# A four-layer mixer trunk on one core: first feed-forward blocks and three mLSTM heads projected down by Strassen's seven products

## The chip, the cores and the metric

The kernel runs on one core of a Trainium2 chip. The metric is the device time of one execution in microseconds, from its start to its end, with all inputs and the output in device memory. The engines are named as in the profile: PE is TensorE (matrix products), PEld its weight loads, DVE is VectorE, ACT is ScalarE, POOL is GpSimd and SP is SyncE, which here only issues DMAs.

## The reference

The trunk has two layers over 512 frames of 1024 features in float32. Each layer is a half-step feed-forward, a mixer, a second half-step feed-forward and a gated embedding, each followed by a residual sum and a layer norm:

```python
x = layer_norm(DN_ALPHA * x + 0.5 * swiglu_ffn(x, ffn1_wgu[i], ffn1_wd[i]), ...)
mix = mlstm_mixer(...) if i % 2 == 0 else gmlp_mixer(...)
x = layer_norm(DN_ALPHA * x + mix, ...)
x = layer_norm(DN_ALPHA * x + 0.5 * swiglu_ffn(x, ffn2_wgu[i], ffn2_wd[i]), ...)
x = layer_norm(DN_ALPHA * x + sigmoid(x @ ple_wg[i] + ple_bg[i]) * (p[i] @ ple_wp[i]), ...)

def swiglu_ffn(x, w_gu, w_d):            # 1024 -> 2 x 2816 -> 1024
    g, u = jnp.split(x @ w_gu, 2, axis=-1)
    return (jax.nn.silu(g) * u) @ w_d
```

The mLSTM mixer of layer 0 projects x to q and k (4 heads of 256 features each, a causal convolution of four taps and silu on them), v and z (4 heads of 512) and eight gate columns. Per head it forms gated causal scores of q and k, multiplies them by v, normalises by the scores' sum and then over the head's 512 features, and gates with norm_g and sigmoid(z). The four heads side by side (2048 features) are multiplied by `w_out` (2048 x 1024). The "down" of this document is the product with `w_d` or `w_out`, whose result is added to the residual stream. The gMLP mixer of layer 1 has a down projection of the same shape, which the change leaves alone.

## The kernel before, in words

**Numbers.** A float32 product is made of three products in the faster type fp32r: each operand is split into a high part and the rest, and `mm3` (L261) issues high x high, low x high and high x low (L263, L264, L265; in the changed kernel the same rows are L268 to L270). `split` (L267) writes the high part by a copy on ScalarE and the low part by a subtraction on VectorE. One "projection" is a weight tile of 128 columns by 1024 rows against all 512 frames, 24 matmuls of 512 columns into one bank of the accumulator memory. There are eight banks, four called "up" and four called "dn"; each pool hands its banks out in turn, and who gets a bank waits until its earlier reader is through.

**Weights.** The class `Weights` streams them in one fixed order for the whole program. A load brings up to 1 MB into a raw buffer (`wraw`, three of them) or, for the feed-forwards' down weights, half that into a quarter buffer (`wquarter`, five). `fill` (L163) then makes the split tiles `whi` (ScalarE) and `wlo` (VectorE; or, where `low="dma"` is passed, a negated copy on ScalarE and an accumulating DMA from GpSimd's queue) in rings of four "main" tiles and some extra ones. `take` hands the next tile to TensorE's code; `release` gives a ring slot back and thereby puts the split of a later tile into the instruction streams of ScalarE and VectorE at that place. `release(later=True)` keeps the slot back until `refill`.

**Order.** No scheduler moves anything: each engine runs its instructions in the order in which the Python code issues them. Engines meet only through semaphores on tiles and banks. So the place of a VectorE instruction in the code decides what it waits behind.

**Feed-forwards.** The 22 blocks of hidden features (128 each) are done in chunks of 2, 4, 4, 4, 4, 4 (`FFN_CHUNKS`). Per block there are two projections (gate and up), then silu and product into `h` or `hf`. The down product of a chunk runs while the next chunk is projected. Chunks 1 to 4 go by Strassen: `Group` views the chunk's `h` and its weights as 2 x 2 blocks and makes seven products, `gps`, one after each of the first seven projections of the next chunk. `form` prepares the left factor of a product (sums of blocks on VectorE, then a split into `fhi` and `flo`), `Weights.forms` the right factor (sums of raw weights in place, then `whi` and `wlo`). `product` runs 12 matmuls into one of two pairs of dn banks, even products into the first pair, odd ones into the second. `add` adds a product's two banks onto the residual `xt`; since products 2, 4, 5 and 6 add onto what already lies in the pair of banks, such a product may start only when the add before it on that pair has read it. The first and the last chunk go by the plain `down` (L591), 12 matmuls per block, frame quarter and pair of halves, tile name `dps`; the first chunk's down stands inside chunk 1 after two projections.

**mLSTM.** Per head: `project_qk` (four projections; per projection bias, convolution by one `TENSOR_SCALAR` L936 and three `SCALAR_TENSOR_TENSOR` L938, silu and a split), `project_v` (four frame quarters, each over four weight tiles, in dn banks), `scores` (24 matmuls into four banks, alternately up and dn; the gate factors `ex` on ScalarE; their product `sf` on VectorE, L1010; a split), two z projections, `mix` (scores times v in `nps`, normalisation up to `hn`, L1049), two more z projections, then the plain down of the head before (96 matmuls, 22 us of TensorE's time) and `gate_turn` (16 transposes into `hps`; product with `sz` into `hzf`, L1067; a split into `hh` and `hl`). In the last head the transposes stand between the frame quarters of that down, and after them comes the last head's own down, joined with the layer norm (`Norm`, whose vectors `g_bc` and `b_bc` have tiles of their own).

## Time and profile before

| | us |
|---|---|
| median of three runs (lowest, highest) | 2247.41 (2246.97, 2248.39) |
| the profiled execution | 2248.24 |
| its span in the trace | 2246.5 |
| first feed-forward (stages by the trace) | 0 to 364 |
| mLSTM | 364 to 778 |
| second feed-forward and embedding | 778 to 1191 |
| third feed-forward | 1191 to 1534 |
| gMLP | 1534 to 1837 |
| fourth feed-forward and embedding | 1837 to 2247 |

The profile is of one execution. A row of the trace in time order has the start and the duration in us, the engine, the line of the code, the instruction, its output and inputs by the program's names, and the shape; `x4` at its end means four such instructions in a row, and then the time is that of all four. A bracket, where there is one, is the idle time of the engine before it and what ended that. A row of the table by windows has the stretch, its length, then busy time and number of instructions in the order PE, PEld, DVE, ACT, POOL, then TensorE's granted clock (1.00 is full speed), the DMA engines' share and their GB/s; columns of engines that did nothing are left out in some rows. A row on waits has the waiting engine and tile, what it waited for, and the total in us, the number of waits and the longest. A row on DMAs has the tile, the queue, the number, the size of each and the median us from issue to landing.

### The profile page before, as it was taken

The numbers are of one execution on the slowest core, as the hardware profiler recorded it, in microseconds if no ns is written. First come the engines' busy times: TensorE is split into PE (matmuls) and PEld (weight loads), VectorE is DVE, ScalarE is ACT, GpSimd is POOL, SyncE is SP. The second block draws the span as 40 slices with busy tenths as digits, with TensorE's granted clock in tenths as the row PEclk, the third lists the DMA queues.
The fourth block names the chain that finished last, engine by engine and source line by source line (L and its number), as shares of the span: only waits on it lengthen the run. The fifth ranks groups of instructions, "written<-read, shape, count | busy, mean of one in ns | idle before, by whom it ended". The sixth has DMA issues, their size and how long they took to land.

```text
span 2246.5 us, 26356 instructions
## 1 busy us (share of the span) xinstructions
PE 2234.0 (99%) x10649; PEld 1875.2 (83%) x10649; DVE 1439.3 (64%) x2083; ACT 886.3 (39%) x1241; POOL 103.2 (5%) x136
## 2 busy tenths in 40 slices
PE   9999999999999999999999999999999999999998
PEld 8888888888888888888889888888888888888887
DVE  5566667765555656666687566666756566666677
ACT  3333336454544433333344333335344452333332
POOL 1000000111121000000000000000010100000000
PEclk9999999999999999999999999999999999999999
DMA  7322223376674534331333332222356453432221
GB/s 237 114 94 93 94 85 100 81 177 123 150 152 106 155 113 131 104 103 57 112 122 122 111 95 95 94 85 94 122 141 141 104 167 98 130 113 85 84 85 57
DMA packets 200754, 254.08 MB, mean 113 GB/s; under 512 B 5636, under 2 KB 155268, under 8 KB 200632
## 3 DMA queue, kind: packets, MB, share of 16 engines
q1 hardware_dynamic: 166864, 211.83, 29.1%
q0 software_dynamic: 27152, 25.87, 7.8%
q10 hardware_dynamic: 6616, 14.69, 2.0%
q8 instruction: 84, 1.38, 0.2%
q14 instruction: 38, 0.31, 0.0%
HBM read 224.58 MB, written 2.11 MB: 101 GB/s over the span
## 4 chain that ended last, share of the span: by engine, by line
PE 97%; DMA 1%; ACT 1%; issue 1%; DVE 0%; SPq 0%; POOL 0%; DVEq 0%; POOLq 0%
PE fps L265 13%; PE fps L263 13%; PE fps L264 13%; PE gps L265 6%; PE gps L263 6%; PE gps L264 6%; PE dps L264 5%; PE dps L265 5%; PE dps L263 5%; PE gups L263 1%; PE zps L263 1%; PE gvps L265 1%; PE zps L265 1%; PE gups L264 1%; PE gups L265 1%; PE zps L264 1%
## 5 line engine op out<-in xcount | busy, mean ns | idle before, releaser
L263 PE MATMUL fps<-xh,whi 128*128 128x512 f32 x1312 | 510.7, 389 | 0.0
L264 PE MATMUL fps<-xl,whi 128*128 128x512 f32 x1312 | 510.5, 389 | 0.0
L265 PE MATMUL fps<-xh,wlo 128*128 128x512 f32 x1312 | 510.4, 389 | 0.0
L194 DVE TENSOR_TENSOR wlo<-wraw,whi 128x1024 fp32r<-128x1024 f32 (+1 forms) x284 | 341.7, 1217 | 183.3 <-ACT whi L188 182.2
L188 ACT ACTIVATE whi<-wraw 128x1024 fp32r<-128x1024 f32 (+1 forms) x333 | 344.2, 1048 | 219.3 <-PE fps L264 103.2
L264 PEld LDWEIGHTS fps<-xl,whi 128*128 128x128 f32 x1312 | 246.3, 188 | 51.2
L265 PEld LDWEIGHTS fps<-xh,wlo 128*128 128x128 f32 x1312 | 246.3, 188 | 51.1
L263 PEld LDWEIGHTS fps<-xh,whi 128*128 128x128 f32 x1312 | 246.3, 188 | 50.9
L194 DVE TENSOR_TENSOR wlo<-wquarter,whi 128x1024 fp32r<-128x1024 f32 x112 | 137.2, 1225 | 202.1 <-ACT whi L188 202.1
L188 ACT ACTIVATE whi<-wquarter 128x1024 fp32r<-128x1024 f32 x112 | 118.7, 1060 | 237.8 <-PE gps L265 177.8
L265 PE MATMUL gps<-whi,flo 128*128 128x512 f32 x448 | 174.3, 389 | 0.0
L264 PE MATMUL gps<-wlo,fhi 128*128 128x512 f32 x448 | 174.3, 389 | 0.0
L263 PE MATMUL gps<-whi,fhi 128*128 128x512 f32 x448 | 174.3, 389 | 0.0
L790 ACT ACTIVATE sg<-fps 128x512 f32<-128x512 f32 x80 | 47.9, 598 | 280.8 <-PE fps L265 280.8
L565 DVE TENSOR_TENSOR xt<-xt,gps 128x512 f32<-128x512 f32 x224 | 143.0, 679 | 0.0
L268 ACT ACTIVATE fhi<-h 128x512 fp32r<-128x512 f32 x112 | 69.4, 625 | 115.9 <-DVE h L726 45.8
L263 PE MATMUL dps<-whi,hh 128*128 128x512 f32 x256 | 101.5, 396 | 0.0
L264 PE MATMUL dps<-wlo,hh 128*128 128x512 f32 x256 | 100.5, 393 | 0.0
L265 PE MATMUL dps<-whi,hl 128*128 128x512 f32 x256 | 100.3, 392 | 0.0
L269 DVE TENSOR_TENSOR flo<-h,fhi 128x512 fp32r<-128x512 f32 x112 | 75.6, 687 | 36.4 <-ACT fhi L268 36.4
L264 PEld LDWEIGHTS gps<-wlo,fhi 128*128 128x128 f32 x448 | 84.1, 188 | 17.5
L263 PEld LDWEIGHTS gps<-whi,fhi 128*128 128x128 f32 x448 | 84.1, 188 | 17.4
(277 smaller groups left out, 3852.4 us busy)
## 6 DMA issues: line engine op xcount, KB each, us to landing
wraw<-in_ffn_wgu_dram SPq DMA_DIRECT2D x79, 1024.0 KB, 5.4
wquarter<-in_ffn_wd_dram SPq DMA_DIRECT2D x64, 512.0 KB, 3.8
wlo<-wraw POOLq DMA_DIRECT2D x49, 512.0 KB, 7.6
wraw<-in_ml_w_in_dram SPq DMA_DIRECT2D x24, 1024.0 KB, 5.7
wraw<-in_gm_w_in_dram SPq DMA_DIRECT2D x15, 1024.0 KB, 5.6
wraw<-in_ffn_wd_dram SPq DMA_DIRECT2D x12, 1024.0 KB, 5.0
wraw<-in_ffn_wgu_dram SPq DMA_DIRECT2D x17, 512.0 KB, 3.9
wraw<-in_ml_w_out_dram SPq DMA_DIRECT2D x8, 1024.0 KB, 5.3
```

The source lines that it names most:

```text
L188: self.nc.scalar.activation(hi[:, s], src[:, s], AF.Copy)
L194: (low or self.nc.vector).tensor_sub(lo[:, s], src[:, s], hi[:, s].bitcast(F32))
L263: mm(ps, st[0], mv[0], start=start, stop=False, skip_group_check=more)
L264: mm(ps, st[0], mv[1], start=False, stop=False, skip_group_check=more)
L265: mm(ps, st[1], mv[0], start=False, stop=stop, skip_group_check=more)
L268: sca.activation(hi, src, AF.Copy)
L269: vec.tensor_sub(lo, src, hi.bitcast(F32))
L565: vec.tensor_add(dst, dst, ps)
L790: sca.activation(sg, ps, AF.Silu)
```

## The change

**Feed-forwards.** Chunk 0 becomes a `Group` too, with two blocks instead of four, so its 2 x 2 blocks are half as large: products of six matmuls, factors of 128 x 256. Its seven products stand after the first seven projections of chunk 1, as those of later chunks do. The first addition to `xt` scales the old residual by ALPHA; so in such a first group the products 0, 2, 3 and 6, which come to each of the four quarters of `xt` first, are added by `SCALAR_TENSOR_TENSOR` instead of `TENSOR_TENSOR`. The affine steps left over from the norm before run at the end of chunk 0 and after the first three projections of chunk 1.

**mLSTM.** Heads 0, 1 and 2 are written by `gate_turn` as plain float32 (`hf`), and a `Group` takes them down during the next head: `step` (add of the product before, the next product, release, next form) stands after the q/k projections 1, 2 and 3, after the v weight tiles 0, 1 and 3, and after the last z projection. The seven weight tiles of `w_out` stand among the head's twelve others by `ML_SLOTS`. One half of a head's `w_out` rows lies in one of the three raw buffers, which are now tracked one by one since they come free out of order, the other in a buffer shared with the norm's `g_bc` and `b_bc`. `project_v` of heads 1 to 3 runs over weight tiles outside and frame quarters inside, with the four up banks; their `scores` use the four up banks too, since the dn banks are pinned by the group. The third z projection moves into `mix` ahead of its last frame quarter. The low parts of z's weight tiles and of the tiles whose raw weights are changed in place no longer go by DMA. Head 3 goes down by the plain `down` with the norm; its transposes stand directly after its last z, with the last product of head 2 between the second and the third of them.

```diff
 class Weights:
-    def forms(self, quarter, kind, raw_kind):
+    def forms(self, kind, b11, b12, b22, b21):
...
+        for _, make in made:
+            self.in_place.add(make)
+        return [(kind, js, make) for js, make in made]
...
-                if low == "dma":
+                if low == "dma" and make not in self.in_place:
...
-                    (low or self.nc.vector).tensor_sub(lo[:, s], src[:, s], hi[:, s].bitcast(F32))
+                    self.nc.vector.tensor_sub(lo[:, s], src[:, s], hi[:, s].bitcast(F32))
...
+    ML_SLOTS = (1, 2, 3, 4, 5, 7, 11)
...
             if h:
-                o_w(h - 1)
-        o_w(HEADS - 1)
+                tiles = W.order[at:]
...
+                j0, j1 = W.add_load(kp(wout)[:, k:k + 2, :], 3), W.add_load(kp(wout)[:, k + 2:k + 4, :], 3, "gb")
...
+                for i, tile_i in enumerate(tiles):
+                    W.order.append(tile_i)
+                    if i in ML_SLOTS:
+                        W.order.append(down_w[ML_SLOTS.index(i)])
+        add_rows(wout, 4 * HEADS - 4, 4)
...
 class Group:
         def add(self):
             r = self.next_add
+            if r == self.next_product:
+                return
             self.next_add += 1
             i, j = self.TO[r]
             for e, ps in enumerate(self.banks[r % 2]):
-                residual(2 * i + e, j, ps, False)
+                residual(2 * i + e, j, ps, r in self.first)
+                if r >= 5:
+                    del pinned[id(ps)]
...
 def ffn:
             for c, n in enumerate(FFN_CHUNKS):
...
-                    if (c, i) in ((0, 3), (1, 0)):
+                    if c == 1 and i < 3:
                         run_affine()
-                    if i == 1 and pending is not None:
-                        down(pending, True)
...
-                if plain:
-                    pending = hs
-                else:
-                    group = Group(h, fpool)
+                if c < LAST:
+                    group = Group(h, fpool, c == 0)
                     group.form()
                     group.form()
+                if c == 0:
+                    run_affine()
...
 def project_qk:
                     W.release(low="dma")
+                    if i:
+                        step()
...
 def project_v:
+                banks = [up_bank("vps") for _ in range(TB)]
+                for k in range(4):
+                    w = W.take()
+                    for t, ps in enumerate(banks):
+                        for kb in (2 * k, 2 * k + 1):
+                            mm3(ps, xs(kb, t * P, (t + 1) * P), [a[:, kb % 2] for a in w], kb == 0, kb == KB - 1)
+                        if k == 3:
+                            take(t, ps)
+                    W.release(low="dma" if k < 2 else None)
+                    if k != 2:
+                        step()
...
 def project_z:
-                W.release(later=i < 2, low="dma")
+                W.release(later=h == 0 or i > 0)
...
 def scores:
-                    ps = (dn_bank if j % 2 else up_bank)("sps")
+                    ps = (dn_bank if j % 2 and h == 0 else up_bank)("sps")
...
 def mix:
-                    bank = up_bank if t >= 2 else dn_bank
+                    if t == 0:
+                        between()
+                    bank = dn_bank if t == 1 else up_bank
...
+            def step(later=False):
+
+                if group is not None:
+                    group.add()
+                    group.product()
+                    W.release(later=later)
+                    group.form()
...
-                if prev is not None:
-                    down(prev, h == 1, low=[None, None, "dma", "dma"] if last else ["dma"] * 4,
-                         between=turn if last else None)
...
+                    group = Group(hs, fpool, h == 0)
+                    group.form()
+                    group.form()
+                    W.refill(4)
+            hs, turn = gate_turn(h, hn, sz)
+            for t in range(TB):
+                turn(t)
+                if t == 1:
+                    step(True)
+                    group.add()
+            W.refill(4)
+            norm = Norm(0, 1)
+            down(hs, False, norm)
```

Three places of the instruction order follow. First, VectorE from the end of a head's mix to the third q/k projection of the next head, before. `hn` is the normalised mix, `wlo` a weight's low part, `sz` the gated norm weight, `acc` the convolution, `ql` the low part of q or k.

```order
L1049 TENSOR_SCALAR hn<-nps,hmv,hr 128x256 x2
L194 TENSOR_TENSOR wlo<-wraw,whi 128x1024 x4
L981 TENSOR_SCALAR sz<-sz,cols 128x512 x2
...
L933 MEMSET pad 128x3
L936 TENSOR_SCALAR acc<-pad,cols 128x512
L938 SCALAR_TENSOR_TENSOR acc<-pad,cols,acc 128x512 x3
L269 TENSOR_TENSOR ql<-acc,qh 128x512
```

And after, the same stretch at the end of head 0. `hf` is now the gated head, `fhi` and `flo` its split factors; L105 to L111 are sums of raw weights, L749 and L750 sums of blocks of the head.

```order
L1109 TENSOR_TENSOR hf<-hps,sz 128x4x128 x4
L274 TENSOR_TENSOR flo<-hf,fhi 128x512 x2
L199 TENSOR_TENSOR wlo<-wraw,whi 128x1024 x2
...
L110 TENSOR_TENSOR wraw<-wraw 128x2x512
L111 TENSOR_TENSOR wraw<-wraw 128x2x512
L199 TENSOR_TENSOR wlo<-wraw,whi 128x1024
L749 TENSOR_TENSOR hf<-hf 128x2x256
L750 TENSOR_TENSOR hf<-hf 128x2x256
L274 TENSOR_TENSOR flo<-hf,fhi 128x512
...
L274 TENSOR_TENSOR ql<-acc,qh 128x512
L586 SCALAR_TENSOR_TENSOR xt<-xt,gps 128x512 x2
```

The factors, the weight sums and their splits now stand between the convolutions of the next head, and the first add onto `xt` (L586) stands behind three of the convolutions.

Second, TensorE from the scores to z in head 1, first row of each bank, before; `sps` are the scores, `zps` is z, and a bracket names the engine whose semaphore the matmul waits on.

```order
L263 MATMUL sps_3980<-qh_3679 128x512 [waits Activation_49]
...
L263 MATMUL sps_4001<-qh_3679 128x384 [waits DVE_49]
...
L263 MATMUL sps_4021<-qh_3679 128x256
...
L263 MATMUL sps_4040<-qh_3679 128x128 [waits DVE_49]
...
L263 MATMUL zps_4065<-xh_87,whi_3798 128x512
```

And after:

```order
L268 MATMUL sps_4180<-qh_3721 128x512 [waits DVE_49]
...
L268 MATMUL sps_4201<-qh_3721 128x384 [waits DVE_49]
...
L268 MATMUL sps_4221<-qh_3721 128x256 [waits DVE_49]
...
L268 MATMUL sps_4240<-qh_3721 128x128 [waits DVE_49]
...
L268 MATMUL zps_4261<-xh_87,whi_4016 128x512 [waits DVE_49]
```

All four scores now wait for VectorE (their banks held v), and so does z, whose bank is that of the first scores; before, z waited for no engine there.

Third, VectorE at the end of head 3, before; `dps` is head 2's down, `hzf` the gated head and `hl` its low part.

```order
L194 TENSOR_TENSOR wlo<-wraw,whi 128x1024 x4
L981 TENSOR_SCALAR sz<-sz,cols 128x512 x2
L565 TENSOR_TENSOR xt<-xt,dps 128x512 x2
L1067 TENSOR_TENSOR hzf<-hps,sz 128x512
L269 TENSOR_TENSOR hl<-hzf,hh 128x4x128
L565 TENSOR_TENSOR xt<-xt,dps 128x512 x2
```

And after:

```order
L199 TENSOR_TENSOR wlo<-wraw,whi 128x1024 x3
L1020 TENSOR_SCALAR sz<-sz,cols 128x512
L1112 TENSOR_TENSOR hzf<-hps,sz 128x512
L274 TENSOR_TENSOR hl<-hzf,hh 128x4x128
L1112 TENSOR_TENSOR hzf<-hps,sz 128x512
L274 TENSOR_TENSOR hl<-hzf,hh 128x4x128
L588 TENSOR_TENSOR xt<-xt,gps 128x512 x2
```

The four gatings of head 3 no longer stand between the quarters of a down of 96 matmuls; the last product's add stands behind two of them.

## The prediction

> **What bounds the kernel now.** First the page: how much of the span TensorE is busy, and who makes up the chain that ended last.

> ```profile
> span 2246.5 us, 26356 instructions
> PE 2234.0 (99%) x10649; PEld 1875.2 (83%) x10649; DVE 1439.3 (64%) x2083; ACT 886.3 (39%) x1241; POOL 103.2 (5%) x136
> PE 97%; DMA 1%; ACT 1%; issue 1%; DVE 0%; SPq 0%; POOL 0%; DVEq 0%; POOLq 0%
> ```

> TensorE is the bound: 12.5 us of 2246.5 are not matmul, and they lie at the two ends. Second view, the waits of TensorE; these are the longest after the first microseconds (us in total, times, longest):

> ```profile
> PE sup L265 <- DVE gbias L494: 0.6, 1, 0.6
> PE vps L264 <- DMA wlo<-wraw: 0.2, 1, 0.2
> ```

> So every matmul taken away is time won, as long as nobody is late for the ones that follow. Third view, the engines by stage (two mLSTM heads, and two stretches of the third feed-forward's first blocks):

> ```profile
> 450.00:551.00 101.00, 101.00 (x489) 85.00 (x488) 57.63 (x120) 48.40 (x71) 14.60 (x17) 1.00 0.62 149
> 652.00:766.00 114.00, 113.75 (x546) 94.97 (x545) 66.25 (x135) 52.43 (x76) 14.95 (x20) 1.00 0.64 144
> 814.00:826.00 12.00, 12.00 (x54) 9.95 (x53) 11.46 (x14) 0.88 (x1) 0.00 (x0) 1.00 0.54 168
> 826.00:846.00 20.00, 20.00 (x90) 16.54 (x89) 5.50 (x5) 5.10 (x6) 0.00 (x0) 1.00 0.14 46
> ```

> The third number of busy time is VectorE: 57.6 of 101 us in a head. It is 43 us short of its limit on average, and the argument below is about the moments at which it isn't.

> **The change: what TensorE saves.** Busy time of the matmuls of `dps` in one first-blocks down and in one head's down, and the first and last matmul of one product of twelve:

> ```profile
> 46.00:58.00 12.00, 11.04 (x48) 9.01 (x48) 5.01 (x8) 1.00 0.56 175
> 528.00:551.00 23.00, 22.56 (x96) 17.98 (x96) 5.05 (x8) 1.00 0.82 183
> 95.63 0.39 PE L263 MATMUL gps<-whi,fhi 128*128 128x512 f32 x1
> 98.12 0.39 PE L265 MATMUL gps<-whi,flo 128*128 128x512 f32 x1
> ```

> A product's matmuls start (98.12 - 95.63) / 11 = 0.226 us apart, so a product of twelve is 2.72 us and a projection of 24 is 5.43. The overhang of a last matmul is 0.39 - 0.23 = 0.16. A head's down is 22.56 - 0.16 = 22.4 us and becomes 84 matmuls or 19.0: 3.4 us each, 10.2 for three heads (if the slower pace of 0.233 belongs to the place, 3 x 12 x 0.233 = 8.4). A first-blocks down is 10.9 and becomes 42 matmuls or 9.5: 1.4 each, 5.5 for four. With the 0.2 of the vps wait that has other weights beside it now: 15.9 us saved, bounds 13.3 and 16.2. [...]

> **What it adds on VectorE.** The rows that price it, in order of time on VectorE (start, us, what; the bracket is the idle time before it):

> ```profile
> 444.17 1.00 DVE L1049 TENSOR_SCALAR hn<-nps,hmv,hr 128x256 f32<-128x256 f32 x2
> 447.64 0.99 DVE L1049 TENSOR_SCALAR hn<-nps,hmv,hr 128x256 f32<-128x256 f32 x2
> 448.55 4.62 DVE L194 TENSOR_TENSOR wlo<-wraw,whi 128x1024 fp32r<-128x1024 f32 x4
> 453.09 0.87 DVE L981 TENSOR_SCALAR sz<-sz,cols 128x512 f32<-128x512 f32 x2
> 454.07 0.69 DVE L1067 TENSOR_TENSOR hzf<-hps,sz 128x512 f32<-128x512 f32 x1
> 455.46 0.69 DVE L269 TENSOR_TENSOR hl<-hzf,hh 128x512 fp32r<-128x512 f32 x1 [0.70 <-ACT hh L268]
> 456.07 0.68 DVE L1067 TENSOR_TENSOR hzf<-hps,sz 128x512 f32<-128x512 f32 x1
> 462.39 0.49 DVE L936 TENSOR_SCALAR acc<-pad,cols 128x512 f32<-128x512 f32 x1 [0.25 <-ACT pad L934]
> 465.19 0.06 DVE L933 MEMSET pad<- 128x3 f32 x1
> 480.70 0.67 DVE L969 TENSOR_TENSOR vf<-vps,vb 128x512 f32<-128x512 f32 x1
> 481.85 0.76 DVE L269 TENSOR_TENSOR vl<-vf,vh 128x256 fp32r<-128x256 f32 x2 [0.48 <-ACT vh L268]
> 550.07 1.39 DVE L563 SCALAR_TENSOR_TENSOR xt<-xt,dps 128x512 f32<-128x512 f32 x2 [4.21 <-PE dps L265]
> 854.79 1.22 DVE L104 TENSOR_TENSOR wquarter<-wquarter 128x1024 f32<-128x1024 f32 x1
> 858.39 1.23 DVE L194 TENSOR_TENSOR wlo<-wquarter,whi 128x1024 fp32r<-128x1024 f32 x1 [1.13 <-ACT whi L188]
> 861.27 1.29 DVE L269 TENSOR_TENSOR flo<-h,fhi 128x512 fp32r<-128x512 f32 x2
> ```

> A low part `wlo` is 1.15 (4.62 / 4), a 512-wide step 0.61 to 0.69, one convolution 2.8 (462.39 to 465.19), a pair of weight sums 2.5, and where a sum is split right away VectorE waits 1.1 for ScalarE. A head now has 14 residual adds for 8, seven operand splits and four operand sums for four splits, four weight sums (4.9 us), and seven tiles of w_out for four, none of whose low parts goes to the DMA. With the low parts that leave the DMA (31 of 49 remain in the program) that is some 20 us more: 78 of 97 us. The average still fits; three places don't, by VectorE's order.

> From the chain of waits, the transposes that end heads 0 and 1, and the start of z in head 1 (start, us, what):

> ```profile
> 450.20 1.75 PE hps L1064 x16
> 499.29 0.29 PE zps L263
> 550.74 1.75 PE hps L1064 x16
> ```

> **Term A, the third product.** Product 2 adds onto the banks of product 0, which VectorE must have read (its first `xt` add). Count from the start of a head's first projection. TensorE gets there after four projections and two products: 4 x 5.43 + 2 x 2.72 = 27.2. VectorE, in head 1, is done with the last `hn` 3.3 us before (447.64 + 0.99 against 450.20 + 1.75), 2.9 with the `sz` that now stands ahead; then come six `wlo` 6.9, one `sz` 0.45, four `hf` 2.45, two `flo` 1.3, three convolutions 8.4, two pairs of weight sums 5.0 with their two `wlo` 2.3 and two waits 2.3, two `ql` 1.3, two operand sums 1.2, their wait 0.7 and `flo` 0.65, and the add 0.7: 33.65. It ends at 30.7, so TensorE waits 3.5. In heads 2 and 3 four `wlo` and the `sz` have gone ahead of the turn: 28.6 from 0.8 before the start, with 0.8 of waiting for the first projection, ends at 28.6: 1.4 each. Sum 6.3. Bounds: without VectorE's four waits 1 in all; with another microsecond at each of them 13.

> Around the scores of head 1: busy time of their matmuls, then ScalarE's and VectorE's rows.

> ```profile
> 495.00:500.00 5.00, 3.92 (x24) 3.72 (x24) 0.00 (x0) 1.00 0.00 0
> 496.93 1.04 ACT L188 ACTIVATE whi<-wraw 128x1024 fp32r<-128x1024 f32 x1
> 497.99 1.28 ACT L1008 ACT_TABLE_LOAD   x1
> 499.28 0.40 ACT L1008 ACTIVATE ex<-ex,reach 128x128 f32<-128x128 f32 x1
> 499.59 0.97 ACT L1008 ACTIVATE ex<-rbc,reach 128x128 f32<-128x128 f32 x3
> 500.60 0.69 DVE L1010 SCALAR_TENSOR_TENSOR sf<-sps,ex 128x512 f32<-128x512 f32 x1 [1.37 <-ACT ex L1008]
> ```

> **Term B, the first z projection.** Before, z starts at 499.29 while `sf` reads the first scores only from 500.60: a different bank, no wait. Now four scores use the four banks of the up pool in turn, and z takes the first one's, so it must wait for `sf`. Also the four values `v` end within one weight tile instead of 5.4 us apart. Count from the start of that last tile: its release of the tile before costs ScalarE 1.05 and VectorE 1.2 (2.4 with the hops), four `vf`, `vl` in series 4 x 1.88 = 7.5 (480.70 to 482.61 is one), so 9.9; ScalarE, free at 9.4, then has two `whi` 2.0, the table 1.3 and the four `ex` 1.3, VectorE two `wlo` and two adds 3.7: 14.0 by the one, 13.6 by the other, then `sf` 0.7: 14.7. TensorE is at z after the tile 5.43, a product 2.72 and the scores 3.76: 11.9. It waits 2.8, in each of three heads: 8.4. Bounds: with the four `v` at VectorE's busy time alone (1.4 each) 0.9 each or 2.7; with a late `whi` 4.5 each or 13.5.

> **Term C, the turn.** The second transpose of heads 1 and 2 takes the bank of the last product, whose add must be through: 0.7 and a hop, 0.5 later than TensorE is there. 1.0 in all, bounds 0 and 2.

> **Term D, the end of head 3.** Before, the transposes of head 3 stood between blocks of head 2's down, 22.4 us of cover. Now VectorE, from 0.9 before the end of the last z, has three `wlo` 3.5, `sz` 0.45, twice `hzf`, wait and `hl` (2.0 each, 454.07 to 456.07), and the last product's add 0.7 until the bank is free in which the final down begins: 7.8 after z. TensorE is there after a product and 16 transposes: 2.72 + 1.75 = 4.5. It waits 3.3, bounds 1 and 5.

> **At nothing: the first chunk of the feed-forwards.** The seven products stand in the eight slots of the second chunk, each now 5.43 + 1.36 us. VectorE loses 16 adds and two splits there, and gains 14 adds and half-sized sums and splits; it was full for 12 us (11.46 above) and then empty (5.50 of 20), and TensorE's next need, product 2, comes some 13 us after the first add can start, with two affine steps and three `wlo` between, about 9. Should that cover go, it is up to 1 us a place: 0 to 4.

> Sum: 6.3 + 8.4 + 1.0 + 3.3 = 19.0 against 15.9: 3.1 us longer. The profiled execution took 2248.24 with a span of 2246.5 and becomes 2251.3; the median of the runs, 2247.41, becomes **2250.5 us**. The bounds reach from 15.9 gained less 4.7 to 13.3 gained less 37; the upper ends hardly come together, so this forecast alone has 2243 to 2258. The waits stand in series on TensorE, with VectorE catching up between them (5 us of idle time ahead of the last v tile, 4 ahead of the mix), so one doesn't pay for another.

> **Rivals.**
> *Cover holds, faster.* VectorE's waits for ScalarE overlap and all terms go to their low ends: 1 + 2.7 + 0 + 1 = 4.7, so 2247.4 - 15.9 + 4.7 = 2236. For it: TensorE showed no wait at all though VectorE was 95% busy for 12 us at 814. Against: there TensorE asked nothing of VectorE; here rows of the order name the wait.
> *Raw weights, slower.* The first rows of w_out hold one of three raw buffers through half a head, and the next z rows must wait for one that a DMA is still reading.

> ```profile
> wlo<-wraw POOLq DMA_DIRECT2D x49, 512.0 KB, 7.6
> wraw<-in_ml_w_in_dram SPq DMA_DIRECT2D x24, 1024.0 KB, 5.7
> ```

> Second v tile split at about 29.5, its low part landed at 38, z's rows at 44; ScalarE wants them at 41.5 and waits 2.5, which VectorE's 5 us ahead of the last v tile takes up. From twice that wait on, each further one costs TensorE: 3.5 a head or 10.5 makes 2261. For it: ScalarE already waits for such rows now and then. Against: the slack.
> *The clock, slower.* TensorE's granted clock is 1.00 in every stage above, and in the one where it idles 9.9 us it is 0.97 over 77:

> ```profile
> 2170.00:2247.00 77.00, 67.11 (x353) 57.34 (x351) 62.35 (x106) 22.24 (x34) 5.70 (x7) 0.97 0.17 62
> ```

> That is 2.3 us lost; if each of the five waits of about 3 us lost as much, 2262. [...]

> **How the numbers follow.** Forecast 0.53, cover 0.28, raw weights 0.14, clock 0.05. 0.2% is 4.5 us (the three runs differ by 0.06%). Faster than 2242.9: cover, and 0.02 of the forecast, 0.30. Slower than 2251.9: both slower rivals and 0.18 of the forecast, 0.37. Between: 0.33. Range: below 2234 lies a third of cover (0.09), above 2261 about half of the two slow rivals (0.10), so **2234 to 2261** holds eight in ten.

> **What would show it.** Matmuls down by 60, `dps` 864 and `gps` of products 1764. TensorE's waits: the third product of heads 1 to 3 on `xt` of VectorE, z on `sf` (about 2.8, three times), the final down on the last add. A head from turn to turn, 100.5 us before (450.20 to 550.74), at 104 for head 1 and 102 for head 2. VectorE near 78 us in a head. Wrong, if TensorE shows no waits for VectorE in the heads and they last 97; or if the waits come from weights by DMA, or from the feed-forwards' second chunk.

## The result and the profile after

The changed kernel takes 2268.28 us (median of five runs, 2267.76 to 2269.23), the kernel before beside it 2248.16; the ratio on record is 1.0094, 95% interval 1.0083 to 1.0105. It is slower by 20 us by the two medians and by 21 by that ratio, where the prediction had 3 us and its range ended at 2261. The profiled execution has a span of 2266.1 against 2246.5.

First the page of the changed kernel, its span, the busy times and the chain of work that ended last:

```profile
span 2266.1 us, 26498 instructions
PE 2234.1 (99%) x10589; PEld 1872.3 (83%) x10589; DVE 1547.6 (68%) x2257; ACT 899.3 (40%) x1281; POOL 84.0 (4%) x118
PE 74%; DVE 5%; ACT 1%; issue 0%; POOL 0%; DVEq 0%; ACTq 0%; POOLq 0%
```

There are 60 matmuls fewer than before, as the change says, and yet TensorE is busy for the same 2234 us: so part of its matmuls must have become slower. VectorE is now in the chain with 5%, where it had 0%. (The shares add up to 80% since the chain is followed back only to 445 us, and a share of the chain is not a wait: VectorE is in it for stretches in which TensorE stood still for only a part.) How long TensorE waits is read from its waits. The waits of TensorE by the profile, the longest:

```profile
PE zps L268 <- DVE sf L1050: 7.6, 3, 2.5
PE dps L268 <- DVE xt L588: 5.5, 3, 3.2
PE gps L268 <- DVE xt L586: 3.8, 1, 3.8
PE gps L268 <- DVE xt L588: 3.7, 2, 1.8
```

These are the terms B (z on `sf`), D (the 3.2 of the second row) and A (the third products of heads 1, 2 and 3) in the places that the prediction named. New are the other two waits in the second row, 1.1 each: they stand at the last chunk of the second and fourth feed-forward. The heads, from turn to turn (columns as before: length, then busy time and count of PE, PEld, DVE, ACT, POOL, then the granted clock, the DMA engines' share and their GB/s):

```profile
447.69:556.59 108.90, 102.56 (x474) 85.37 (x473) 79.02 (x145) 48.94 (x72) 8.98 (x12) 0.95 0.40 112
556.59:662.40 105.81, 101.45 (x473) 84.65 (x472) 75.72 (x141) 48.27 (x71) 9.01 (x12) 0.97 0.39 105
```

A head was 100.5 us and was to be 104 and 102; it is 108.9 and 105.8. VectorE's 78 us a head were right. What was not forecast is the clock: 0.95 and 0.97 where it had been 1.00. Three stretches around head 2's third product, for TensorE alone (length, busy time and count, clock, DMA share, GB/s), show how that comes about:

```profile
585.53:588.94 3.41, 1.58 (x7) 1.00 0.30 58
588.94:592.36 3.42, 3.42 (x9) 0.50 0.51 96
592.36:595.77 3.41, 3.41 (x16) 1.00 0.91 217
```

The wait of 2.0 us lies in the first stretch. In the second the granted clock is 0.50, and 9 matmuls start where 16 do in the third, at 1.00 again. In the changed kernel's trace there are eight such windows of 3.41 us at 0.50 before the last matmul, all behind waits of the mLSTM, and none before the last matmul in the kernel before. By these rows each costs about half its length: 8 x 1.71 = 13.7 us, an estimate that takes each as busy throughout, which the first, busy for 2.28 of 3.41, is not.

So the theory to be tested is a ledger: the saving, less the waits for VectorE, less half a window for each halved one. Its rivals: the half clock belongs to the place or to VectorE's load and not to idling; and VectorE has simply too much to do in a head, so that a wait taken away in one place comes back in another.

### The profile page after: what moved, and what is told of

Its sections match the earlier page's. It is cut to its first block, busy times and chain, and to the rows that moved or that the text cites. A ratio compares the mean times of both kernels' runs of the same rounds, so it can differ in the third digit from the quotient of the medians.

```text
span 2266.1 us, 26498 instructions
## 1 busy us (share of the span) xinstructions
PE 2234.1 (99%) x10589; PEld 1872.3 (83%) x10589; DVE 1547.6 (68%) x2257; ACT 899.3 (40%) x1281; POOL 84.0 (4%) x118
## 3 DMA queue, kind: packets, MB, share of 16 engines
q8 instruction: 83, 1.36, 0.2%
## 4 chain that ended last, share of the span: by engine, by line
PE 74%; DVE 5%; ACT 1%; issue 0%; POOL 0%; DVEq 0%; ACTq 0%; POOLq 0%
PE fps L269 10%; PE fps L270 10%; PE fps L268 10%; PE gps L268 6%; PE gps L270 6%; PE gps L269 6%; PE dps L268 3%; PE dps L269 3%; PE dps L270 3%; PE gups L268 1%; PE gups L269 1%; PE gups L270 1%; PE gvps L270 1%; PE gvps L268 1%; PE gvps L269 1%; DVE wlo L199 1%
## 5 line engine op out<-in xcount | busy, mean ns | idle before, releaser
L268 PE MATMUL fps<-xh,whi 128*128 128x512 f32 x1312 | 510.7, 389 | 0.0
L269 PE MATMUL fps<-xl,whi 128*128 128x512 f32 x1312 | 510.4, 389 | 0.0
L199 DVE TENSOR_TENSOR wlo<-wquarter,whi 128x1024 fp32r<-128x1024 f32 (+1 forms) x140 | 156.6, 1118 | 218.1 <-ACT whi L193 218.1
L268 PEld LDWEIGHTS fps<-xh,whi 128*128 128x128 f32 x1312 | 246.3, 188 | 51.0
L269 PEld LDWEIGHTS fps<-xl,whi 128*128 128x128 f32 x1312 | 246.3, 188 | 50.8
L193 ACT ACTIVATE whi<-wquarter 128x1024 fp32r<-128x1024 f32 (+1 forms) x140 | 136.3, 974 | 279.7 <-PE gps L270 208.9
L268 PE MATMUL gps<-whi,fhi 128*128 128x512 f32 x588 | 231.4, 394 | 7.5 <-DVE xt L586 3.8
L270 PE MATMUL gps<-whi,flo 128*128 128x512 f32 x588 | 231.6, 394 | 0.0
L269 PE MATMUL gps<-wlo,fhi 128*128 128x512 f32 x588 | 231.2, 393 | 0.0
L588 DVE TENSOR_TENSOR xt<-xt,gps 128x512 f32<-128x512 f32 x282 | 180.4, 681 | 0.5 <-PE gps L270 0.5
L268 PEld LDWEIGHTS gps<-whi,fhi 128*128 128x128 f32 x588 | 111.5, 190 | 32.0 <-ACT whi L193 8.7
L273 ACT ACTIVATE fhi<-h 128x512 fp32r<-128x512 f32 (+1 forms) x140 | 80.5, 581 | 142.9 <-DVE h L750 54.4
L270 PEld LDWEIGHTS gps<-whi,flo 128*128 128x128 f32 x588 | 111.5, 190 | 23.8
L269 PEld LDWEIGHTS gps<-wlo,fhi 128*128 128x128 f32 x588 | 111.6, 190 | 23.6
L274 DVE TENSOR_TENSOR flo<-h,fhi 128x512 fp32r<-128x512 f32 (+1 forms) x140 | 87.2, 635 | 42.9 <-ACT fhi L273 42.9
L461 ACT ACTIVATE xf<-xps,cols 128x128 f32<-128x128 f32 x160 | 59.9, 454 | 57.0 <-PE xps L456 56.9
## 6 DMA issues: line engine op xcount, KB each, us to landing
wraw<-in_ffn_wgu_dram SPq DMA_DIRECT2D x79, 1024.0 KB, 6.3
wquarter<-in_ffn_wd_dram SPq DMA_DIRECT2D x64, 512.0 KB, 3.7
wraw<-in_ml_w_in_dram SPq DMA_DIRECT2D x24, 1024.0 KB, 5.9
wlo<-wraw POOLq DMA_DIRECT2D x31, 512.0 KB, 6.4
wraw<-in_gm_w_in_dram SPq DMA_DIRECT2D x15, 1024.0 KB, 5.6
wraw<-in_ffn_wgu_dram SPq DMA_DIRECT2D x17, 512.0 KB, 3.9
wraw<-in_ffn_wd_dram SPq DMA_DIRECT2D x8, 1024.0 KB, 4.9
wraw<-in_ml_w_out_dram SPq DMA_DIRECT2D x8, 1024.0 KB, 5.0
```

The source lines that it names most:

```text
L193: self.nc.scalar.activation(hi[:, s], src[:, s], AF.Copy)
L199: self.nc.vector.tensor_sub(lo[:, s], src[:, s], hi[:, s].bitcast(F32))
L268: mm(ps, st[0], mv[0], start=start, stop=False, skip_group_check=more)
L269: mm(ps, st[0], mv[1], start=False, stop=False, skip_group_check=more)
L270: mm(ps, st[1], mv[0], start=False, stop=stop, skip_group_check=more)
L273: sca.activation(hi, src, AF.Copy)
```

## The experiments

All fourteen are variants of the changed kernel, except the two ladders, which are variants of the kernel before. In the table, "idle" is the sum of TensorE's pauses after the first 30 us (start to start of two matmuls, where that is over 0.6 us, less 0.227), "half" the number of halved windows ahead of the last matmul, "last" the start of that matmul in the trace, and "saved" what the ledger then gives: (2236.83 - 0.41) + idle + 1.71 x half - last, where 2236.83 and 0.41 are the last matmul and the idle time of the kernel before. The intervals are those on record.

| kernel | median us | ratio to before, 95% | idle | half | last | saved |
|---|---|---|---|---|---|---|
| changed | 2268.28 | 1.0094 (1.0083-1.0105) | 21.55 | 8 | 2256.66 | 15.0 |
| fill | 2256.67 | 1.0044 (1.0029-1.0059) | 2.58 | 1 | 2247.31 | - |
| a_slots | 2262.14 | 1.0068 (1.0051-1.0085) | 20.05 | 5 | 2250.52 | 14.5 |
| b_bank | 2279.05 | 1.0142 (1.0126-1.0157) | 34.99 | 8 | 2267.37 | 17.7 |
| b_bank2 | 2252.73 | 1.0027 (1.0017-1.0037) | 13.81 | 4 | 2241.70 | 15.4 |
| d_banks | 2261.51 | 1.0062 (1.0047-1.0077) | 17.59 | 5 | 2248.39 | 14.2 |
| all3 | 2247.95 | 1.0003 (0.9994-1.0013) | 9.44 | 3 | 2236.98 | 14.0 |
| all4 | 2252.86 | 1.0024 (1.0014-1.0034) | 12.00 | 5 | 2242.97 | 14.0 |
| early | 2256.03 | 1.0038 (1.0024-1.0051) | 14.06 | 5 | 2245.18 | 13.9 |
| early_all4 | 2239.97 | 0.9971 (0.9960-0.9982) | 5.84 | 0 | 2228.47 | 13.8 |
| early_bd | 2236.57 | 0.9953 (0.9941-0.9966) | 2.82 | 0 | 2225.47 | 13.8 |
| ffn_only | 2244.67 | 0.9989 (0.9979-0.9999) | 2.58 | 0 | 2233.29 | 5.7 |
| ffn_d | 2241.46 | 0.9975 (0.9965-0.9984) | 0.53 | 0 | 2230.51 | 6.4 |

The last column lies between 13.8 and 15.4 for nine kernels with the whole change, whose times differ by 32 us: that the sum closes so nearly is the ledger's main support. (In fill the pauses are filled with matmuls, so it says nothing there, and its one halved window lies at 11.9 us, in the start. In b_bank four of the eight halved windows are busy for only 4.75 of 13.64 us; the low clock has no matmuls to slow in the idle part, so 1.71 is too much there, and b_bank's 17.7 stands apart.)

Some 0.8 to 1.4 of each figure in that column is not the change's doing. In the trace of the kernel before, the first projection of the first feed-forward (`fps`) starts at 30.18; in the others, fill apart, it starts at 28.8 to 29.4, and in the two ladders, whose code is that of the kernel before up to there, at 29.4. So that one execution was late at its start. Counted from that projection on, the nine kernels saved 12.5 to 14.0, the changed one 13.8, early_bd 13.0 and ffn_d 5.6.

**fill: the pauses filled.** It tells whether the half clock follows from idling.

```diff
+                    if h and j == TB - 1:
+                        for _ in range(14):
+                            mm(ps[:, P:], xh[:, 0, :P], xh[:, 0, P:], start=True, stop=True)
...
+            def busy(n):
+                ps = up_bank("fill")
+                for _ in range(n):
+                    mm(ps, xh[:, 0, :P], xh[:, 0], start=True, stop=True)
...
 def step:
                     group.add()
+                    if group.next_product == 2:
+                        busy(16 if group.first else 8)
                     group.product()
...
+            busy(14)
```

> The changed kernel, with extra matmuls of 0.227 us whose results nobody reads where TensorE idled in the mLSTM: 16 ahead of head 1's third product (idle 3.97 us), 8 in heads 2 and 3 (2.0 each), 14 narrower ones ahead of the first z of heads 1 to 3 (2.6 each), 14 after the last transposes (3.3). VectorE's lateness stays as it is. Clock theory (the half clock in 8 windows of 3.41 us follows from TensorE's idle time): all windows at full clock, 8 x 1.71 = 13.7 us less, 2254.6, and the granted clock 1.00 in the mLSTM. Rival (the half clock belongs to the place, to VectorE's or the DMAs' load, not to idle time): 2268 to 2270 with the same windows at 0.5.

It took 2256.67. The mLSTM of fill by heads, the same stretches as the prediction showed of before:

```profile
450.00:551.00 101.00, 100.78 (x488) 84.66 (x487) 75.57 (x141) 48.11 (x71) 8.97 (x12) 1.00 0.43 120
551.00:652.00 101.00, 100.95 (x488) 84.72 (x488) 74.72 (x139) 48.22 (x71) 8.46 (x11) 1.00 0.41 110
```

VectorE is as late as in the changed kernel: its first add onto `xt` ends 31.3 us after head 1's first matmul and 29.3 after that of heads 2 and 3, in both traces alike. TensorE does nothing more that is of use, and the clock is 1.00. The time is 11.6 us less, with matmuls that nobody needs. With the pauses filled the heads' clock is 1.00, where the changed kernel's was 0.95 and 0.97: the half clock comes from idling, and the first rival falls.

**a_slots: products one slot later.**

```diff
-    ML_SLOTS = (1, 2, 3, 4, 5, 7, 11)
+    ML_SLOTS = (1, 2, 4, 5, 6, 7, 11)
...
-                    if i:
+                    if i in (1, 2):
                         step()
...
-                    if k != 2:
-                        step()
+                    step()
```

> The changed kernel with the third to sixth product and their weights one slot later: nothing after the fourth q/k projection, one after each of the four v weight tiles. Wait-and-clock theory: the third product's waits go (3.97 + 2.0 + 2.0 us) with 4 windows at half clock (6.8), 2268.3 - 14.8 = 2253.5. Rival 1 (half clock not from idling): 2268.3 - 8.0 = 2260.3 with 8 windows still at half. Rival 2 (VectorE is simply overloaded in a head, the lateness turns up at the next product or at z): 2265 to 2268, with new waits of the same sum in the v tiles.

A miss, at 2262.14. Its waits:

```profile
PE zps L268 <- DVE sf L1049: 9.4, 3, 3.1
PE dps L268 <- DVE xt L588: 5.5, 3, 3.2
PE vps L268 <- ACT pad L953: 4.2, 3, 1.4
```

The third product's waits went, as expected. But a product behind the fourth projection had covered something else: the v tiles take that projection's bank, which ScalarE had not yet read (`pad`). And z's waits grew from 2.5 to 3.1 each, probably since the product after the third v tile now brings VectorE and ScalarE work there. The three pauses at `vps`, 1.56 us each by the matmuls' starts, did not halve the clock. That the time lies near the first rival's 2260.3 is chance: the halved windows fell from 8 to 5, and the new waits made up for it.

**b_bank and b_bank2: a bank for z.** The scores of 256 and of 128 columns fit into one bank, so three banks do for four scores.

```diff
-                    ps = (dn_bank if j % 2 and h == 0 else up_bank)("sps")
+                    if h and j == 3:
+                        ps = res[2][2][:, 256:]
+                    else:
+                        ps = (dn_bank if j % 2 and h == 0 else up_bank)("sps")
...
```

> The changed kernel with the two narrow scores (256 and 128 columns) of heads 1 to 3 in one bank, so that the first z projection gets a bank of its own. Wait-and-clock theory: z's waits for sf go (3 x 2.6 us) with 3 windows at half clock (5.1): 2268.3 - 12.8 = 2255.5. Rival 1 (half clock not from idling): 2260.6. Rival 2 (lateness moves on, to the second z or to the mix): 2265 to 2268.

```profile
PE sps L268 <- DVE sf L1053: 20.6, 3, 6.9
PE gps L268 <- DVE xt L586: 3.8, 1, 3.8
```

The first form was slower by 11 us, for a reason that neither theory had: the fourth scores' matmuls are issued after VectorE's read of the third scores, and since both lie in one bank now, they wait for that read, 6.9 us in each head. b_bank2 issues the matmuls of both before the first read:

```diff
...
                 for j in range(TB):
...
+                    if not h or j < 3:
+                        product(j)
+                    if h and j == 2:
+                        product(3)
...
```

> The changed kernel with the two narrow scores of heads 1 to 3 in one bank as in b_bank, but with the matmuls of both issued ahead of VectorE's first reading of that bank, so that no matmul waits for a reader there. Wait-and-clock theory: z's waits for sf go (3 x 2.6 us) with 3 windows at half clock (5.1): 2268.3 - 12.8 = 2255.5. Rival (VectorE is overloaded and the lateness moves on, to the second z or the mix): 2265 to 2268.

2252.73: z's waits are gone, and no other wait of the heads has grown. It is 2.8 us better than the ledger's figure, of which 1.7 are a halved window fewer: of the two pauses of 2.0 us in heads 2 and 3, which both halved the clock in the changed kernel, one does so here and one does not.

**d_banks: the order of the dn banks.**

```diff
                 if r >= 5:
-                    del pinned[id(ps)]
+                    at = pinned.pop(id(ps))
+                    dn_order.remove(at)
+                    dn_order.append(at)
```

> The changed kernel in which the dn banks are handed out in the order in which the group frees them, so that the plain down behind a group begins in the banks of product 5 and not in those of product 6, the last. Wait-and-clock theory: the wait at the end of head 3 shrinks from 3.3 to about 1 us (the gated head is then the last to come), its half-clock window goes (1.7), and the two waits of 1.3 at the last chunk of the second and fourth feed-forward go: 2268.3 - 2.3 - 1.7 - 2.6 = 2261.7. Rival (these waits are for VectorE itself, whichever bank): 2267 to 2268.

```profile
PE zps L268 <- DVE sf L1052: 7.6, 3, 2.5
PE gps L268 <- DVE xt L586: 3.8, 1, 3.8
PE gps L268 <- DVE xt L588: 3.7, 2, 1.8
PE xps L456 <- DVE xt L565: 1.8, 1, 1.8
```

2261.51, where 2261.7 was expected. The three waits of `dps` are gone, the two of the feed-forwards among them; a wait of 1.8 in the norm of head 3's down takes the place of one of 3.2. That the time comes out so exactly is partly luck: in the trace (of an execution that took 2259.53) the window at the end of head 3 is still halved, which was to go, and three of the four behind the third products are not, which were to stay.

**ffn_only and ffn_d: the feed-forwards' part alone.** The mLSTM, its weights' order and its plain down are those of the kernel before.

> The feed-forwards' part of the change alone: mLSTM, its weights' order and the plain down as before. By the ledger: 24 matmuls fewer, 5.5 us, and at the last chunk of the second and fourth feed-forward two waits of 1.3: 2247.0 - 5.5 + 2.6 = 2244.1, or 2241.5 if the banks fall so that these waits don't come; no half clock. Rival (VectorE's cover in chunk 1 doesn't hold): 2247 or more, with waits of the products in chunk 1.

> ffn_only with the dn banks handed out in the order in which the group frees them: the feed-forwards' part alone, without the two waits at the last chunk. 2244.7 - 2 x 1.29 = 2242.1; rival (the waits are for VectorE, whichever bank): 2244.7.

```profile
PE dps L268 <- DVE xt L583: 2.3, 2, 1.1
```

That is the only longer wait of ffn_only (2244.67), and with the banks' order of d_banks it is gone: 2241.46, faster than before by 5.6 us. No product of chunk 1 waits for VectorE in either.

**all3, all4: all three mended, with other slots.** all3 is b_bank2 and d_banks with the products after the projections 2 and 3 and all v tiles, all4 after 1 and 3 and all v tiles (`ML_SLOTS` 2, 3, 4, 5, 6, 7, 11 and 1, 3, 4, 5, 6, 7, 11).

> The changed kernel with three things undone: products 0 to 5 of a head one by one after the q/k projections 2 and 3 and the four v weight tiles (so 8.15 us lie between product 0 and product 2 and the start of the head has none); the scores' banks as in b_bank2; the dn banks' order as in d_banks. Wait-and-clock theory: all waits go (8.0 + 7.7 + 3.3 + 2.6 = 21.6 us) with all half-clock windows (13.7): 2268.3 - 35.3 = 2233.0, up to 2236 with what little is left of the waits; faster than the kernel before. Rival (VectorE's load in a head is what costs, and its lateness turns up elsewhere): 2245 to 2260, with new waits of TensorE for VectorE in the heads.

> As all3, but the products 0 and 1 of a head stand after the q/k projections 1 and 3 (2 to 5 after the four v weight tiles): between product 0 and product 2 lie two more projections' worth than in all3 (19.0 us against 13.6), and the product after the fourth q/k projection covers ScalarE's reading of that projection's bank, for which the v tiles of a_slots waited 1.4 us. Wait-and-clock theory: the three waits of all3 (2.34 each) and its three half-clock windows (1.71 each) go: 2248.0 - 7.0 - 5.1 = 2235.9, no half-clock window but the one at the end, faster than the kernel before by 11. Rival (VectorE's lateness turns up elsewhere, as it did three times so far): 2243 to 2248.

Both missed: 2247.95 and 2252.86, and here the second rival came nearer. The third product still waited, 2.3 us in each head in all3 and 3.2 in all4. In all3 as much TensorE work lay between the first product and the third as in the changed kernel (two projections and a product, 13.6 us; the 8.15 of its expectation leaves out a projection). In all4 it was a projection more, and the wait grew all the same. VectorE in all4's head 1 in order of time shows why:

```profile
480.65 1.23 DVE L199 TENSOR_TENSOR wlo<-wraw,whi 128x1024 fp32r<-128x1024 f32 x1 [1.13 <-ACT whi L193]
481.82 0.06 DVE L954 MEMSET pad<- 128x3 f32 x1
481.99 0.49 DVE L957 TENSOR_SCALAR acc<-pad,cols 128x512 f32<-128x512 f32 x1
482.51 2.32 DVE L959 SCALAR_TENSOR_TENSOR acc<-pad,cols,acc 128x512 f32<-128x512 f32 x3
484.76 0.68 DVE L274 TENSOR_TENSOR ql<-acc,qh 128x512 fp32r<-128x512 f32 x1
485.36 1.28 DVE L586 SCALAR_TENSOR_TENSOR xt<-xt,gps 128x512 f32<-128x512 f32 x2
```

The first add (last row) belongs to `step`, and `step` stands behind the convolution of its projection. Whoever moves the second product later moves the first add behind a later convolution. So either VectorE's load or this order was to blame, and that could be told apart.

**early: the add ahead of the convolution.** The same work on every engine; only the add's place in VectorE's order changes, in `project_qk`.

```diff
                     ps = banks.popleft() if banks else project()
+                    if group is not None:
+                        group.add()
```

> The changed kernel with one thing moved: in the q/k projections of heads 1 to 3, VectorE's add of the product before stands ahead of the convolution instead of behind it (about 3.5 us earlier in VectorE's order, with exactly the same work). Order theory (the third product waits since the first add stands behind a convolution, not since VectorE has too much to do in a head): its waits of 3.97, 2.0 and 2.0 us shrink to 0.5, 0 and 0, and 4 half-clock windows go: 2268.3 - 7.4 - 6.8 = 2254.1. Load theory (VectorE's total lateness is what counts): the convolutions are then late by as much, for the scores or for z, and the time stays at 2264 to 2268.

```profile
PE zps L268 <- DVE sf L1052: 7.6, 3, 2.5
PE dps L268 <- DVE xt L588: 5.5, 3, 3.2
PE gps L268 <- DVE xt L586: 0.6, 2, 0.3
```

2256.03: the products' waits of 7.5 us are down to 0.6, all in head 1 (0.2 at the third product, 0.3 at the fifth), while z and the end of head 3 wait as before to the tenth. The 1.9 us above the ledger's figure are one halved window more at the end of head 3. In head 1 VectorE's rows are now, against an add at 480.03 in the changed kernel:

```profile
475.68 0.69 DVE L274 TENSOR_TENSOR flo<-hf,fhi 128x512 fp32r<-128x512 f32 x1 [0.70 <-ACT fhi L273]
476.29 1.28 DVE L586 SCALAR_TENSOR_TENSOR xt<-xt,gps 128x512 f32<-128x512 f32 x2
478.22 2.33 DVE L959 SCALAR_TENSOR_TENSOR acc<-pad,cols,acc 128x512 f32<-128x512 f32 x3
```

**early_bd, early_all4: everything mended.** early_bd is early with b_bank2 and d_banks, early_all4 is all4 with the early add.

> early with the scores' banks of b_bank2 and the dn banks' order of d_banks; slots as in the changed kernel. Order theory: from b_bank2, 2252.7, less the third products' waits 7.5, less 3.3 + 2.6 of the banks plus 1.8 that d_banks showed in their place, less 4 half-clock windows 6.8: 2234.3, to 2237 if a window is halved at the end of the mLSTM; faster than the kernel before by 10 to 13. Load theory: 2243 to 2250 with new waits.

> all4 with the adds ahead of the convolutions as in early. Order theory: the first add stands two projections ahead of the third product and its wait goes altogether: 2252.9 - 3 x 3.35 - 4 half-clock windows 6.8 = 2236.0, one window at the end of the mLSTM still halved. Load theory: 2248 to 2253.

early_bd took 2236.57, faster than the kernel before by 10.5 us (ratio 0.9953, interval 0.9941 to 0.9966), and is the best of all. Its longest waits after the start, and its first two heads from turn to turn:

```profile
PE xps L456 <- DVE xt L565: 1.8, 1, 1.8
...
PE gps L268 <- ACT whi L193: 0.3, 1, 0.3
447.91:546.80 98.89, 98.32 (x473) 82.15 (x472) 78.90 (x145) 48.50 (x72) 8.19 (x12) 1.00 0.45 123
546.80:644.62 97.82, 97.82 (x474) 82.30 (x472) 75.64 (x141) 47.92 (x71) 8.22 (x12) 1.00 0.42 113
```

VectorE is busy for 78.9 and 75.6 us there, and for 79.0 and 75.7 in the changed kernel: the same load, in heads that are 10.0 and 8.0 us shorter. The load theory falls; the order of the work and of the banks was to blame. early_all4, 2239.97 where 2236.0 was expected, still has the `pad` waits of a_slots (1.1 each), though its slots put a product behind the fourth projection to cover them; why that isn't enough was not followed further.

**ladder, ladder2: pauses of known length.** Pauses are set into feed-forwards of the kernel before, by a chain of small steps between a matmul and a transpose.

> The kernel before with twelve pauses of TensorE in the first and third feed-forward, two in each of chunks 2 to 4: a matmul, a chain of 3 to 22 small VectorE steps on its result, and a transpose that waits for them, so idle times of about 1 to 5 us; their results are not used. Window theory (fixed windows of 3.41 us; the one after a window that was idle for more than about half runs at half clock): pauses up to 1.7 us never halve the clock, pauses of 2 to 3.4 some by where they fall, pauses over 3.7 always; time is 2247 plus the pauses plus 1.7 us per halved window. Rival (only pauses longer than a whole window of 3.4 us count): none of 1.8 to 3.3 us halves it.

> The kernel before with twelve shorter pauses of TensorE, in the middle of projections of the first and third feed-forward, made by a chain of 1 to 13 small ScalarE steps between a matmul and a transpose, so idle times of about 0.8 to 4 us; their results are not used. Window theory as the runs so far have it (the window of 3.41 us after one that was idle for more than 0.57 to 0.64 of it runs at half clock; at half clock the next one stays so from 0.17 to 0.18 on): no pause under 1.9 us halves the clock, one of 1.9 to 3.9 does when enough of it falls into one window, one of over 3.9 always does; each halved window costs 1.7 us. Rival (a single gap counts by its length, from 2 us on): all from 2 us on halve it, wherever they fall.

In the first, VectorE's other work stood ahead of the chain and all twelve pauses were 3.4 to 10 us long; 24 windows were halved, which tells little. In ladder2, with ScalarE's steps, they were 0.4 to 4.5 us (the profile's own idle times, 0.16 less than by the table's measure). None of the six up to 2.07 halved the clock; 2.42, 3.10, 3.78 and 4.46 did; 2.75 and 3.44 did not. Two of these, by windows on the grid of the halved ones:

```profile
1299.60:1303.01 3.41, 0.99 (x6) 1.00 0.85 270
1303.01:1306.42 3.41, 3.41 (x10) 0.50 0.55 183
1398.58:1401.99 3.41, 1.49 (x7) 1.00 0.76 261
1401.99:1405.40 3.41, 1.89 (x9) 1.00 0.00 0
1405.40:1408.82 3.42, 3.42 (x17) 1.00 0.00 0
```

The pause of 2.42 us lies in one window, which is busy for 0.99 of 3.41, and the next is halved. The longer pause of 3.44 is divided between two windows, busy for 1.49 and 1.89, and neither is followed by a halved one. The expectation that a pause over 1.9 us depends on where it falls holds, and the rival, that length alone decides, falls.

## Why the prediction was wrong

**Right, in mechanism and nearly in size.** The feed-forwards' part: 5.5 us forecast, 5.6 measured by ffn_d, and chunk 1 hides its work on VectorE. The places of the waits: A 6.3 forecast and 8.0 measured (3.97, 2.0, 2.0, start to start less 0.227), B 8.4 and 7.7 (3 x 2.58), D 3.3 and 3.3. VectorE's load in a head was 78 us and is 79 and 76. The raw weights, a rival at 0.14, show in no wait of the changed kernel's list.

**Right in kind, off in size.** The saving: 15.9 forecast, about 13 by the ledger counted from the first projection on, just under the forecast's lower bound of 13.3. The feed-forwards' part held, so the mLSTM's was too large: 10.2 forecast, 7.4 by early_bd less ffn_d (13.0 - 5.6). The figure with the place's slower pace of 0.233, 8.4, was nearer; the last microsecond was not followed. Term C, 1.0, was not there at all.

**Missing.** The bank in which the plain down of the last chunk begins was not looked at: two waits of 1.3 us. "At nothing" was said of chunk 1 only, and the end of the same feed-forward was left out; d_banks shows that this is the pinned banks' order and not VectorE's load.

**The step that failed** is the half clock, which has no term in the forecast's sum. It stood at nothing there and comes to 13.7 us by the trace (8 x 1.71; filling the pauses gained 11.6), two thirds of the whole loss. It was seen, in the rival on the clock: "if each of the five waits of about 3 us lost as much, 2262", with a chance of 0.05. So a clock lost to idling was there, with a price, but kept out of the forecast. The length of a wait alone does not tell whether it halves the clock: waits of 2.0 us did in heads 2 and 3, and a pause of 3.44 us in ladder2 did not. With eight windows at 1.71 the forecast's sum becomes 3.1 + 13.7 = 16.8; with 2.1 less saved (13.8 for the changed kernel, against 15.9) and the 2.6 at the last chunks 21.5; C's 1.0 that did not come and the 1.0 that A and B were longer together cancel. Measured: 20.1 by the medians, 21 by the ratio.

A second fault lay beside it. The row with a clock of 0.97 in the kernel before was read as 2.3 us lost to idling in the last stage. TensorE in the end of that stretch, cut finer:

```profile
2200.00:2237.00 37.00, 37.00 (x209) 1.00 0.12 44
2242.05:2246.50 4.45, 0.00 (x0) 0.50 0.31 118
```

The half clock begins at 2242.05, behind the last matmul: it cost nothing, and it was no measure of what a pause between matmuls costs. The rival's 2262 was near the 2268 in size, but by a price (2.3 us a wait) that no run shows; the runs show 1.71 a window. The place of the halved stretch has to be looked at, not its mean over 77 us.

What the prediction said of cover was too coarse as well. It counted VectorE's chain to the third product nearly rightly (a wait of 3.5 us for 3.97 in head 1, 1.4 for 2.0 in the others), and took it as given. The chain was long because of one instruction's place: 3.5 us of it were a convolution and a split ahead of an add that didn't need them.

## What to carry to other kernels

When TensorE waits, price the wait twice: its own length, and half of a window of 3.41 us for every window that this puts at half clock. Here that took an idle share of about 0.6 in the window before (7 of 13 between 0.56 and 0.62, all 42 above), and a wait well below 1.9 us cost only itself. Before calling an engine overloaded, look at what stands ahead of the one instruction that is waited for, and in which bank the waiting one begins: with the same work, three such places were worth 32 us of 2268. And a piece of work that is moved may have been the cover of something else, as the product behind the fourth projection was in a_slots.

## What the runs showed of the hardware

| window at | idle share | windows | next one at half |
|---|---|---|---|
| full clock | 0.10 to 0.56 | 50 | 0 |
| full clock | 0.56 to 0.62 | 13 | 7 |
| full clock | over 0.62 | 42 | 42 |
| half clock | up to 0.17 | 11 | 0 |
| half clock | 0.17 to 0.19 | 2 | 2 |
| half clock | over 0.19 | 20 | 20 |

(At full clock 16 more windows were idle for 0.10 or less, and none of them halved the next. In the other six traces no window after the first 30 us and ahead of the last matmul is idle for over 0.57, and none is at half clock.)

So no pause up to 0.56 x 3.41 = 1.9 us halved the clock here, wherever it lay; one over 2 x 0.62 x 3.41 = 4.2 fills more than 0.62 of some window, and all 42 such windows were followed by one at half clock. Behind a halved window the clock was 1.00 again in all 11 cases where that window was idle for up to 0.17 of its length, and in none of the 22 above: head 1's wait of 3.97 us reached 1.1 us into a second window, a third of it, and two windows were halved for it. Of pauses between these bounds it depended on how they fell on the grid: of 2.0 us in the same two places, both halved the clock in the changed kernel, one in b_bank2 and none in d_banks.

The speed of the faster type shows in the trace of the kernel before: at a granted clock of 1.00 the matmuls in fp32r start 0.227 us apart at 512 columns (`fps`) and 0.120 at 256 (`sup`), and the transposes in float32 0.109 at 128 (`hps`).
